# Issuing the scan's inverse and off-diagonal loads from GpSimd instead of SyncE, in a bidirectional DeltaNet / attention / MoE layer

## The chip, the cores and the metric

The kernel runs on one core of a Trainium2 chip. The metric is the device time of one execution, in microseconds (us): the median of three runs of the kernel before is 1728.37 us (1728.33 to 1729.34). The engines are TensorE (PE; PEld is its loading of weights), VectorE (DVE), ScalarE (ACT), GpSimd (POOL) and SyncE (SP). SP does no arithmetic; it issues transfers (DMAs). DMAs can also be issued by ACT and by POOL, and each of these engines works through its own instructions strictly in order.

## The reference

One layer of an encoder trunk, batch 1, 1024 tokens, width 1024, all in float32:

```python
h = rmsnorm(x) * (1 + scale1) + shift1            # shifts, scales, gates from silu(c) @ W_ada + b_ada
proj = h @ w_in                                   # attention q k v, DeltaNet q k v z, beta, decay, gates
A = block_attention(rope(q), rope(k), v)          # 8 query heads, 2 key heads, dim 64
B = gated_delta(fwd) + flip(gated_delta(bwd))     # 8 heads, dim 64, chunks of 64 tokens, 16 chunks
#   per chunk: T = inverse(I + L);  v_new = T@(b*(v - eg*k@state));  o = eg*q@state + a@v_new
#              state = gl*state + k^T@v_new       # sequential over the chunks
x = x + gate1 * ((sig(gA)*(A@Wa) + sig(gB)*(B'@Wd)) @ w_o)
x = x + gate2 * expert_choice_moe(rmsnorm(x) * (1 + scale2) + shift2)   # 16 experts, 128 tokens each
```

## The kernel before, in words

Large products are made of three matmuls over a high and a low part of each operand. The stages follow each other in this order: the first norm and its modulation, the projections for the DeltaNet, per-chunk matrices, the inversion of the 32x32 diagonal blocks on VectorE (`dn_invert`), the scan (about 370 to 715 us), the attention (to about 875 us), the up-projections with `w_o` and the routing, and the 16 experts.

**The scan.** `scan` runs 16 steps; step t treats chunk t forward and chunk 15 - t backward together. `scan_step` has the matmuls of lines 654, 669, 684 and 691 and the VectorE operations between them (658 to 693); line 687 writes the new state `Sc`, which line 654 of the next step needs. `scan_merge` puts the inverse of a chunk together from 32x32 blocks: line 630 multiplies an off-diagonal block (`nf`, loaded from `n_d`) with a transposed inverse (`wt`, from `wt_d`), line 637 multiplies the result with the inverse `w` (from `w_d`), line 639 writes it back into `w`, and line 669 uses `w`. The merge for step t + 1 runs within step t.

**Its loads.** `scan_load(t)` issues for each of the two directions two transfers of `w`, one of `nf` and one of `wt` (32 KB each, 256 pieces of 128 bytes), then in its second half `kq`, `kv` and `at`. For step t + 2 it is called in step t. `w` has two buffers; consecutive steps use different halves of the partitions of `nf` and `wt`. In the trace the tiles `nf` and `wt` share one allocation and are both named `Sc`; `w` is named `W`.

**What fills TensorE.** `late_fill` is a stream of 672 matmuls (line 1209: 14 groups of 48, for the remaining gates), of which `scan` hands out some after each part of a step, 35 a step as written:

```python
FILL = 8, 9, 9, 9, 60
```

Each group needs 512 KB of `w_in` (`wraw`, line 284, issued by POOL), which ACT (line 290) and VectorE (line 291) split into `wh` and `wl`. `attn_prep` (normalised and rotated q and k, one tile of 128 tokens a step, lines 739 to 809) runs beside steps 0 to 8; its `rope` table `tab` is multiplied on POOL (line 750). `mods_late` (lines 910 to 947; 40 VectorE operations of lines 930 and 932, each on a 256 KB load of `w_ada` issued by SP) comes behind it, and `scan_post` follows each step from step 8 on. After step 8, `attn_load` has POOL load 3.5 MB of keys, queries and values (lines 816 to 820).

**What sets the order.** The program is written in one order, but a scheduler puts each engine's instructions into the order in which, by its own estimates, they become ready. It also adds the waits. Each DMA of SP and ACT takes the next of eight counters, each DMA of POOL the next of eight others, and a DMA that takes a counter waits for the DMA that had it before.

Of the kernel before, what the change touches and what calls it, by code (L numbers as in the profile page):

```python
# [85 lines left out]
class K:  # L86
# [511 lines left out]
    def scan_load(self, t):  # L598


        nc = self.nc
        w = self.W[t % 2]
        nf, at, kv = self.nf, self.sa[:, t % 2], self.kv[t % 2]
        quads, ns = [], (t, 15 - t)
        kq = [self.kqs[d][:, t % 2] for d in range(2)]
        for d, n in enumerate(ns):
            x = n % 2
            src = self.w_d[d].rearrange("(n h) (b s c) -> n b s h c", h=8, b=2, s=32)
            for b in range(2):
                nc.sync.dma_start(w[64 * x + 32 * b:64 * x + 32 * b + 32, :, b * 32:b * 32 + 32], src[n, b])  # L610
            f, o = slice(64 * x + 32 * d, 64 * x + 32 * d + 32), slice(64 * x + 32 - 32 * d, 64 * x + 64 - 32 * d)
            nc.sync.dma_start(nf[f], self.n_d[d, n].rearrange("h s c -> s h c"))
            nc.sync.dma_start(self.wt[f], self.wt_d[d].rearrange("(n h) (c s) -> n c h s", h=8, s=32)[n])
            quads.append((f, o, slice(32 * d, 32 * d + 32), slice(32 - 32 * d, 64 - 32 * d)))
        yield w, at, kv, kq, nf, quads
        for d, n in enumerate(ns):
            r = slice(64 * (n % 2), 64 * (n % 2) + 64)
            nc.sync.dma_start(kq[d], self.kq_d[n])
            nc.sync.dma_start(kv[r], self.kv_d[n // 2, r])
            nc.sync.dma_start(at[r].rearrange("p h c -> p (h c)"), self.a_d[d, n // 2, r])  # L620
        yield
# [1065 lines left out]
```

## Time and profile before

| | |
|---|---|
| median of three runs | 1728.37 us |
| the profiled execution | 1728.42 us, its span 1726.6 us |
| granted TensorE clock, mean | 0.967 of full speed |
| busy: PE, DVE, ACT, POOL | 94%, 82%, 53%, 12% of the span |
| DMA traffic | 388.8 MB, 225 GB/s on average |

A timeline row gives start and length of a piece of work on an engine, and in brackets how long the engine had been idle and what ended that. In a row of windows, PEclk is the granted clock of TensorE as a share of full speed (1.0 is 2.4 GHz, 0.5 is 1.2 GHz), averaged over the stretch, and the DMA share is the mean busy share of the 16 DMA engines. "SPq" is SP's own queue of instructions.

### The profile page before, as it was taken

How to read it: one execution, taken by the hardware profiler on the slowest of the kernel's cores; microseconds unless marked ns; L12 is line 12 of the kernel's file. 1: busy time of each engine (PE TensorE's matmuls, PEld its weight loads, DVE VectorE, ACT ScalarE, POOL GpSimd, SP SyncE). 2: the span in 40 equal slices, each digit the busy share in tenths (PEclk: the TensorE clock that was granted, in tenths of full speed). 3: DMA queues.
4: the chain of work that ended last, by engine and by line, in shares of the span. 5: the costliest groups of instructions: out<-in, count | busy, mean ns of one | idle time of the engine just before them, and what ended most of it. 6: DMA issues, size and time to landing. Idle time of an engine off the chain costs nothing. (4 is left out here: it accounts for less than half of the span.)

```text
span 1726.6 us, 30147 instructions
## 1 busy us (share of the span) xinstructions
PE 1616.8 (94%) x11131; PEld 1278.1 (74%) x11131; DVE 1409.3 (82%) x2470; ACT 907.1 (53%) x1352; POOL 204.3 (12%) x196
## 2 busy tenths in 40 slices
PE   6999999889999899699999999669999999999997
PEld 4777778677777677478887788557777777777786
DVE  6899897954667757789986567979999999999996
ACT  6654432122344213288871323347777777777775
POOL 0000022010100100021112312300011000110000
PEclk9999999998999999699999999879999999999999
DMA  9454377257778966721135464769999999999981
GB/s 280 129 175 131 104 181 195 82 179 171 184 197 225 273 176 182 196 86 38 38 111 182 155 209 147 259 227 351 384 379 374 382 388 383 375 377 384 385 309 25
DMA packets 284146, 388.81 MB, mean 225 GB/s; under 512 B 88219, under 2 KB 152399, under 8 KB 283487
## 3 DMA queue, kind: packets, MB, share of 16 engines
q1 hardware_dynamic: 263279, 325.54, 57.4%
q0 software_dynamic: 14096, 48.77, 10.3%
q10 hardware_dynamic: 6624, 12.59, 2.0%
q8 instruction: 88, 1.44, 0.4%
q14 instruction: 59, 0.48, 0.1%
HBM read 328.04 MB, written 58.77 MB: 224 GB/s over the span
## 5 line engine op out<-in xcount | busy, mean ns | idle before, releaser
L1576 DVE TENSOR_TENSOR ew<-er,ew 128x1024 fp32r<-128x1024 f32 x384 | 452.2, 1219 | 29.8 <-ACT ew L1575 29.7
L1575 ACT CAST ew<-er 128x1024 fp32r<-128x1024 f32 x384 | 391.0, 1049 | 137.9 <-PE pj L1629 105.4
L1629 PE MATMUL pj<-ew,xT 128*128 128x512 f32 x1536 | 367.6, 396 | 4.5 <-DVE ew L1576 4.5
L1629 PEld LDWEIGHTS pj<-ew,xT 128*128 128x128 f32 x1536 | 283.2, 188 | 76.2 <-DVE ew L1576 19.5
L1646 PE MATMUL tr<-ew,aT 128*128 128x512 f32 x768 | 191.3, 398 | 0.0
L1646 PEld LDWEIGHTS tr<-ew,aT 128*128 128x128 f32 x768 | 139.7, 188 | 30.4 <-DVE ew L1576 3.4
L297 PE MATMUL pj<-hTh,wl 128*128 128x512 f32 (+1 forms) x384 | 123.4, 399 | 6.5 <-DVE wl L279 6.5
L297 PE MATMUL pj<-hTh,wh 128*128 128x512 f32 (+1 forms) x384 | 122.0, 397 | 3.3 <-ACT hTh L258 1.8
L297 PE MATMUL pj<-hTl,wh 128*128 128x512 f32 (+1 forms) x384 | 121.5, 397 | 1.4 <-DVE hTl L261 1.4
L297 PEld LDWEIGHTS pj<-hTh,wl 128*128 128x128 f32 (+1 forms) x384 | 71.9, 188 | 23.7 <-DVE wl L279 6.9
L297 PEld LDWEIGHTS pj<-hTh,wh 128*128 128x128 f32 (+1 forms) x384 | 70.7, 187 | 20.6 <-ACT hTh L258 1.9
L866 DVE TENSOR_REDUCE am<-pj 128x1 f32<-128x1024 f32 x64 | 77.7, 1216 | 10.0 <-PE pj L861 9.5
L1652 POOL DMA_INDIRECT out_dram<-xe,idxT x16 | 37.2, 2327 | 407.9 <-DVE tok L1550 353.4
L297 PEld LDWEIGHTS pj<-hTl,wh 128*128 128x128 f32 (+1 forms) x384 | 71.2, 187 | 18.6 <-DVE hTl L261 2.0
L1255 PE MATMUL pj<-hTh,uw 128*128 128x512 f32 x256 | 83.5, 404 | 1.0 <-DVE uth L1261 0.5
L868 ACT ACTIVATE ap<-pj,am 128x1024 f32<-128x1024 f32 x64 | 71.8, 1123 | 20.7 <-DVE am L866 11.1
L1209 PE MATMUL pj<-hTh,wh 128*128 128x512 f32 x224 | 79.9, 423 | 0.8 <-ACT y L1214 0.8
L1209 PE MATMUL pj<-hTh,wl 128*128 128x512 f32 x224 | 79.4, 422 | 0.0
L1209 PE MATMUL pj<-hTl,wh 128*128 128x512 f32 x224 | 77.8, 416 | 0.0
L861 PE MATMUL pj<-kT,qT 128*128 128x512 f32 x256 | 76.3, 406 | 0.0
L278 ACT CAST wh<-wraw 128x1024 fp32r<-128x1024 f32 (+1 forms) x26 | 26.7, 1028 | 87.9 <-PE pj L297 87.9
L325 DVE SCALAR_TENSOR_TENSOR y<-xc,colt,y 128x1024 f32<-128x1024 f32 x48 | 61.4, 1279 | 1.4 <-ACT y L323 0.9
(391 smaller groups left out, 2899.0 us busy)
## 6 DMA issues: line engine op xcount, KB each, us to landing
er<-in_w_gate_dram SPq DMA_DIRECT2D x128, 512.0 KB
er<-in_w_up_dram SPq DMA_DIRECT2D x128, 512.0 KB
er<-in_w_down_dram SPq DMA_DIRECT2D x128, 512.0 KB
wraw<-in_w_in_dram POOLq DMA_DIRECT2D x36, 512.0 KB, 5.9
mw<-in_w_ada_dram SPq DMA_DIRECT2D x44, 256.0 KB
wt<-in_w_ada_dram SPq DMA_DIRECT2D x16, 512.0 KB
gate_d<-y ACTq DMA_DIRECT2D x32, 256.0 KB
kqs<-kq_d SPq DMA_DIRECT2D x32, 256.0 KB
```

Source lines behind the costliest of these rows:

```text
L297: self.nc.tensor.matmul(ps[q][:n], w[:, k, :n], x[k][:, q * 512:(q + 1) * 512], start=(k == 0 and w is wh and x is self.hTh), stop=(k == 7 ...
L325: nc.vector.scalar_tensor_tensor(y, xc[:, t:t + S], w(t), y, op0=OP.mult, op1=OP.add)
L861: nc.tensor.matmul(ps[:, kh], qT[:, i * 128:(i + 1) * 128], self.kT[a][:, s, kh * 512:(kh + 1) * 512], start=(s == 0), stop=(s == 1), skip ...
L866: nc.vector.reduce_max(m, ps, axis=AX.X, negate=True)
L868: nc.scalar.activation(p, ps, AF.Exp, bias=m, scale=1.0, accum_out=self.rv[:, h, half * 4 + i:half * 4 + i + 1])
L1209: nc.tensor.matmul(ps[q], a[:, k], x[k][:, q * 512:(q + 1) * 512], start=(k == 0 and a is wh and x is self.hTh), stop=(k == 7 and a is wl))
L1255: nc.tensor.matmul(ps, w[:, k], v[k][:, qs], start=(k == 0 and p == 0), stop=(k == 3 and p == 2))
L1575: nc.scalar.copy(hi, raw)
L1576: nc.vector.tensor_sub(lo, raw, hi.bitcast(F))
L1629: nc.tensor.matmul(pg[m], x[:, 2 * kp + k], wi[:, k], start=(kp == 0 and k == 0 and n == 0), stop=(kp == 3 and k == 1 and n == 2))
L1646: nc.tensor.matmul(py[q], x[:, k], wi[:, q], start=(k == 0 and n == 0), stop=(k == 7 and n == 2))
L1652: nc.gpsimd.indirect_dma_start(out=out2, out_offset=bass.IndirectOffsetOnAxis(ap=self.idx[:, e:e + 1], axis=0), in_=y, in_offset=None, com ...
```

## The change

The four transfers per direction of `scan_load`'s first half are issued by POOL (`nc.gpsimd`) in place of SP (`nc.sync`): 8 a step, 128 in all. Their addresses and sizes stay.

```diff
--- before.py
+++ after.py
@@ -607,10 +607,10 @@
             x = n % 2
             src = self.w_d[d].rearrange("(n h) (b s c) -> n b s h c", h=8, b=2, s=32)
             for b in range(2):
-                nc.sync.dma_start(w[64 * x + 32 * b:64 * x + 32 * b + 32, :, b * 32:b * 32 + 32], src[n, b])
+                nc.gpsimd.dma_start(w[64 * x + 32 * b:64 * x + 32 * b + 32, :, b * 32:b * 32 + 32], src[n, b])
             f, o = slice(64 * x + 32 * d, 64 * x + 32 * d + 32), slice(64 * x + 32 - 32 * d, 64 * x + 64 - 32 * d)
-            nc.sync.dma_start(nf[f], self.n_d[d, n].rearrange("h s c -> s h c"))
-            nc.sync.dma_start(self.wt[f], self.wt_d[d].rearrange("(n h) (c s) -> n c h s", h=8, s=32)[n])
+            nc.gpsimd.dma_start(nf[f], self.n_d[d, n].rearrange("h s c -> s h c"))
+            nc.gpsimd.dma_start(self.wt[f], self.wt_d[d].rearrange("(n h) (c s) -> n c h s", h=8, s=32)[n])
             quads.append((f, o, slice(32 * d, 32 * d + 32), slice(32 - 32 * d, 64 - 32 * d)))
         yield w, at, kv, kq, nf, quads
         for d, n in enumerate(ns):
```

The scheduler also gives other engines another order. The rows below are each engine's own sequence.

TensorE at the end of the scan, before: from line 691 of step 14 to the first transposes of the attention (`ap`).

```order
L691 MATMUL dn<-st,sa 64x64 x16
L630 MATMUL tr<-Sc 32x32 x16
L684 MATMUL tr<-st,kv 64x64 x8
L654 MATMUL dn<-Sc,kqs 64x64
L637 MATMUL tr<-W,pt 32x32 x16
L654 MATMUL dn<-Sc,kqs 64x64 x31
L945 MATMUL tr<-macc,ones 1x512
L669 MATMUL dn<-st,W 64x64 x13
L149 MATMUL tr<-masks,st 128x128 x4
L669 MATMUL dn<-st,W 64x64 x3
L691 MATMUL dn<-st,sa 64x64 x16
L149 MATMUL dn<-masks,ap 128x128 x16
```

The same place now, from line 654 of the last step to its line 691:

```order
L654 MATMUL dn<-Sc,kqs 64x64 x26
L1209 MATMUL pj<-hTl_489,wh 128x512
L1209 MATMUL pj<-hTh_488,wl 128x512 x2
L1209 MATMUL pj<-hTh_529,wh 128x512 x2
L1209 MATMUL pj<-hTl_530,wh 128x512 x2
L1209 MATMUL pj<-hTh_529,wl 128x512 x2
L669 MATMUL dn<-st,W 64x64 x16
L1209 MATMUL pj<-hTh_570,wh 128x512 x2
L1209 MATMUL pj<-hTl_571,wh 128x512 x2
L1209 MATMUL pj<-hTh_570,wl 128x512 x2
L1209 MATMUL pj<-hTh_611,wh 128x512 x2
L691 MATMUL dn<-st,sa 64x64 x16
```

Before, the fill (line 1209) is used up when the last two steps run; now each step keeps about 35 of the 672, and 72 come after the last line 669. The steps in which the order before had more are, by the count of line 1209 between two lines 669, step 1 to 2 (76), 10 to 11 (57) and 11 to 12 (62). The four scores (line 861), which stood between steps 12 and 14, now stand behind the last step, 12 or 13 fills apart.

POOL around `attn_load`, before:

```order
L284 DMA wraw<-in_w_in_dram 128x8x128
L750 TENSOR_TENSOR tab<-rp,rw 128x128 x2
L284 DMA wraw<-in_w_in_dram 128x8x128
L816 DMA kT_6104<-kT_d 128x2x1024
L818 DMA qT_6106<-qT_d 128x512
L818 DMA qT_6107<-qT_d 128x512
L819 DMA vS<-vS_d 128x8x256
L820 DMA kT_6105<-kT_d 128x2x1024
L284 DMA wraw<-in_w_in_dram 128x8x128
```

and now:

```order
L612 DMA Sc<-n_d 32x8x32
L613 DMA Sc<-wt_d 32x8x32
L816 DMA kT_6104<-kT_d 128x2x1024
L818 DMA qT_6106<-qT_d 128x512
L818 DMA qT_6107<-qT_d 128x512
L819 DMA vS<-vS_d 128x8x256
L820 DMA kT_6105<-kT_d 128x2x1024
L610 DMA W<-w_d 32x8x32 x4
L612 DMA Sc<-n_d 32x8x32
L613 DMA Sc<-wt_d 32x8x32
L612 DMA Sc<-n_d 32x8x32
L613 DMA Sc<-wt_d 32x8x32
```

What moved: the four loads of `w` for step 11 and the `nf` and `wt` of step 12 stand behind `attn_load`; in front of it are the `w` of step 10 and the `nf` and `wt` of step 11. Two loads of `wraw` that stood before the first `tab` now stand behind the loads for steps 0 to 2, and from there on a `wraw`, a pair of `tab` or both stand between the loads of most steps and the next. On VectorE, 16 of the 40 operations of `mods_late` now stand in steps 1 to 3, beside `attn_prep`; before, all stood in step 8 and later.

## Rows read from the trace of the kernel before

**Rows 1.** The page: busy tenths of TensorE in 40 equal slices of the span.

```profile
PE   6999999889999899699999999669999999999997
```

**Rows 2.** Windows of the scan: us, PE, PEld, DVE, ACT, POOL busy, PEclk, DMA share, GB/s.

```profile
382.50:390.00 7.50, 2.58 (x8) 1.33 (x6) 0.77 (x2) 0.60 (x1) 0.66 (x1) 0.79 0.84 168
390.00:400.00 10.00, 9.35 (x89) 6.55 (x93) 0.00 (x0) 1.48 (x4) 0.87 (x2) 0.50 1.01 201
...
466.70:541.90 75.20, 72.63 (x1125) 56.49 (x1125) 53.62 (x146) 32.62 (x72) 6.21 (x11) 1.00 0.81 216
566.00:574.00 8.00, 7.88 (x104) 6.75 (x104) 6.32 (x19) 4.08 (x7) 0.00 (x0) 0.79 0.62 167
598.00:606.00 8.00, 0.55 (x4) 0.15 (x3) 3.39 (x14) 0.53 (x1) 0.00 (x0) 0.75 0.89 258
606.00:612.00 6.00, 6.00 (x16) 4.51 (x15) 0.75 (x1) 0.00 (x0) 0.00 (x0) 0.50 0.93 241
690.00:730.00 40.00, 24.56 (x319) 17.34 (x315) 30.55 (x68) 8.43 (x16) 0.00 (x0) 0.66 0.73 191
```

**Rows 3.** Timeline of PE: start, length, line, tile, [idle before <-releaser].

```profile
387.12 0.28 PE L630 MATMUL tr<-Sc 32*32 32x32 f32 x2 [4.32 <-DMA Sc<-wt_d]
...
390.65 1.02 PE L630 MATMUL tr<-Sc 32*32 32x32 f32 x30 [1.25 <-DMA Sc<-wt_d]
...
605.90 0.28 PE L630 MATMUL tr<-Sc 32*32 32x32 f32 x2 [7.45 <-DMA Sc<-wt_d]
...
693.45 0.68 PE L684 MATMUL dn<-st,kv 64*64 64x64 f32 x16 [2.94 <-DVE st L674]
```

**Rows 4.** Waits of SP's queue, 360 to 400 us: us in total, times, longest.

```profile
SPq L613 <- DMA rw<-in_k_norm_w_dram: 2.2, 1, 2.2
SPq L612 <- DMA rw<-in_k_norm_w_dram: 2.0, 1, 2.0
```

**Rows 5.** Timeline of SP: start, length, line, transfer.

```profile
592.53 4.40 SPq L612 DMA_DIRECT2D Sc<-n_d  x1
```

**Rows 6.** Line 610's DMAs on SP: ns min/median/max, first and last start.

```profile
L610 SPq DMA_DIRECT2D W<-w_d x64: 303/443/1682, 377.2 to 694.9; - x64
```

**Rows 7.** Line 525's DMAs on POOL, and their landing.

```profile
L525 POOL DMA_DIRECT2D n_d<-nn x32: 582/582/600, 226.4 to 293.3; - x32
...
DMA to landing us min/median/max: 1.9/2.9/5.7
```

**Rows 8.** Windows again: the stretch in which line 525 issues.

```profile
200.00:300.00 100.00, 99.27 (x891) 78.31 (x891) 84.95 (x159) 29.96 (x48) 23.88 (x38) 1.00 0.67 169
```

**Rows 9.** DMA issues on POOL: KB each, median us to landing.

```profile
wraw<-in_w_in_dram POOLq DMA_DIRECT2D x36, 512.0 KB, 5.9
...
kT<-kT_d POOLq DMA_DIRECT2D x2, 1024.0 KB, 10.2
```

**Rows 10.** Timeline of POOL: the first load of attn_load, and a `wraw`.

```profile
587.27 0.70 POOL L816 DMA_DIRECT2D kT<-kT_d  x1 [11.10 <-DMA st<-in_w_ada_dram]
...
596.92 0.90 POOL L284 DMA_DIRECT2D wraw<-in_w_in_dram  x1 [6.22 <-DVE wl L291]
```

**Rows 11.** Waits over the whole span: us in total, times, longest.

```profile
POOL wraw L284 <- DVE wl L291: 81.3, 6, 18.6
```

**Rows 12.** Timeline of PE: starts of line 669 in steps 4, 5, 9, 10.

```profile
486.61 1.15 PE L669 MATMUL dn<-st,W 64*64 64x64 f32 x32
...
505.45 1.15 PE L669 MATMUL dn<-st,W 64*64 64x64 f32 x32
...
574.60 1.15 PE L669 MATMUL dn<-st,W 64*64 64x64 f32 x32
...
589.07 1.15 PE L669 MATMUL dn<-st,W 64*64 64x64 f32 x32
```

**Rows 13.** Line 930 on DVE, and a wait before it.

```profile
L930 DVE SCALAR_TENSOR_TENSOR macc<-mw,cs,macc x15: 732/744/751, 566.1 to 717.7; 128x512 f32<-128x512 f32 x15
...
  DMA st<-in_w_ada_dram: 5.7, 1
```

## The prediction

> **What bounds the kernel now.** I read the slices of the whole span first. Each is 43.2 us; apart from the first and the last, TensorE is under nine tenths in six of them: the eighth, ninth, 14th and 17th (302 to 388, 561 to 604, 690 to 734 us), which hold the scan's beginning, middle and end, and the 26th and 27th, ahead of the experts [rows 1]. Then I read windows of the scan, then TensorE's own timeline for what ended its idle times, and last the queues of SP and POOL for what had been late.
>
> In the middle of the scan TensorE is the bound: 72.6 us of 75.2 are busy at full clock, while VectorE is busy for 53.6 [rows 2]. What can be won lies in four places where TensorE stands idle or, just after, is granted less than the full clock. I count a place as its idle time plus busy time times the missing share of the clock, all from [rows 2]:
>
> - start, 382.5 to 400: 4.92 + 2.58 x 0.21 + 0.65 + 9.35 x 0.50 = 10.8 us;
> - 566 to 574: 0.12 + 7.88 x 0.21 = 1.8 us;
> - 598 to 612: 7.45 + 0.55 x 0.25 + 6.00 x 0.50 = 10.6 us;
> - end of the scan and start of the attention, 690 to 730: 15.44 + 24.56 x 0.34 = 23.8 us.
>
> Together 47.0 us. At the first and the third place the wait is for a load of the scan: line 630 waits 4.32, 1.25 and 7.45 us for `wt` [rows 3]. At the end it is not: line 684 of the last steps waits for VectorE (2.94 us) [rows 3], because no fill is left to lie between a step's links. The clock rows show the same order each time: TensorE stood still, and afterwards worked at a granted 0.50 (1.2 GHz) for six to ten us [rows 2].
>
> Why the loads are late can be read on SP. Two of the first loads waited 2.2 and 2.0 us for transfers of `rw` that have nothing to do with them [rows 4]: the wait for the counter that the earlier transfer still holds. Before the wait at 605.90 one issue alone took SP 4.40 us [rows 5], where a load of this size usually takes 0.44 [rows 6].
>
> **What leaves SP.** 128 issues x 0.443 us = 57 us of SP [rows 6]. Nothing computes on SP, so this is worth nothing by itself; it counts only through loads that start earlier, and these are in the places above.
>
> **What comes to POOL.** No row shows such a load issued from POOL. The nearest is the store of `n_d`, the same 256 pieces of 128 bytes in the other direction: 582 ns each [rows 7]. I take it; 128 x 0.582 = 74.5 us, 4.7 us a step. From both sides: not below the 0.30 us of SP's shortest [rows 6], and as an upper end the 0.90 us of a `wraw` with its 512 KB [rows 10], 38 to 115 us in all. A step lasts 18.84 us in the first half (35 fills, from step 4 to 5) and 14.47 us with 31 fills in the second (from step 9 to 10) [rows 12], so POOL has room at either end, and I charge nothing. The landing I bound by 2.9 us (`n_d`, [rows 7]) and 10.2 us (1 MB of `kT`, [rows 9]) and take 2.9, nearest in size.
>
> A rule speaks against this place. VectorE was busy for 85 of the 100 us in which most of the 32 stores of `n_d` were issued, and their issue stayed within 582 to 600 ns [rows 7, 8]. The Trainium skill (DMA: Bandwidth & Descriptors, SWDGE vs HWDGE vs iDMA) says that GpSimd writes the descriptors of its DMAs into SBUF and can be locked out there by VectorE in some modes, which SP's DMAs are immune to. By that rule the issues would lengthen beside a busy VectorE; these rows show no lengthening, and the sum keeps 582 ns.
>
> **The four places, one by one.**
>
> Start. POOL's last load for step 0 stands behind the store of `wt_d`, as on SP, but not behind `rw` or `kq`. The place costs between 0 (all landed in time) and 10.8 us (as late as before). With five issues of 0.58 us and 2.9 us landing instead of SP's waits I take 2.
>
> 598 to 612. The load that was late was `wt`, issued on SP among other transfers, while the attention's 3.5 MB moved. Now the `nf` and `wt` of step 11 stand before `attn_load` in POOL's order, and behind it only the `w` of step 11 and the `nf` and `wt` of step 12. Three of the `w` can be issued at once; the next waits for the counter of the first 1 MB load, 10.2 us [rows 9]. Issue and landing of five loads behind the last 1 MB load, which may end some 3 us later than 10.2 because five issues precede it, make about 10 + 3 + 5 x 0.58 + 2.9 = 19 us. The first use of `w`, line 637 of step 11, comes, by the order of the matmuls, about a step and two thirds after POOL is through with step 10's loads (an estimate: 14.47 x 1.67 = 24 us), and the `nf` of step 12 a step later still. So I take 0; the upper end is the old 10.6. In that row the first of these loads itself had waited 11.10 us [rows 10], and now the `w` of step 11 would wait with it: that is the upper end's case.
>
> Order of TensorE. The fill is spread at about 35 a step to the last step, and 72 lie behind it with the scores between them. The total of matmuls is the same. In the last two steps fill lies where the idle time was; behind them the attention still has to start: its first exponentials, transposes and the last `scan_post` follow each other. Of the 23.8 us I keep a third, 8 (between 0 and 23.8).
>
> First steps. In steps 1 to 3 VectorE gets 16 operations of `mods_late` at 0.744 us [rows 13]: 11.9 us in three steps, beside 53.6 / 4 = 13.4 a step [rows 2]. That makes 17.4 a step against 18.84 [rows 12], so VectorE gets as full as TensorE and the order decides; I take 2 us a step, 6 (0 to 11.9). The same 11.9 us are missing in steps 8 to 15, where that gives VectorE air but no time, for TensorE bounds there.
>
> Small waits, with the 1.8 us at 566, go on in the new order: 5 (0 to 10).
>
> **The sum.** 47.0 - (2 + 0 + 8 + 6 + 5) = 26 us less. From the profiled execution's 1728.42 us (span 1726.6 and 1.8 around it; 0.05 above the median, so nothing has to be converted): 1702.4, I say 1702. Every stage behind the scan keeps its length: the later stages have the same instructions, and a shift of the scan's end shifts them whole. With the lower ends of all terms it would be 1681, with the upper ends (10.8 + 10.6 + 23.8 + 11.9 + 10 = 67) 1748; all of them at one end is unlikely.
>
> **Rivals.**
>
> *The loads stay late.* If a load takes from POOL as long as the transfers around it, the start (10.8) and the wait beside the attention's loads (10.6) stay, and only the order gains: 47.0 - (10.8 + 10.6 + 8 + 6 + 5) = 6.6, so 1722. For it: both waits fell into stretches with the DMA engines 84 to 101% busy [rows 2], and POOL's 1 MB loads took 10 us there [rows 9]. Against it: 4.40 us of issue and the waits on `rw` were SP's own [rows 4, 5]. The Trainium skill says the same as this rival (DMA: Bandwidth & Descriptors, Issuing engines are not separate DMA queues): the DMAs of all issuers share 16 engines, and a second issuer saves only issue time. By that rule alone the 57 us of SP's issue would be the whole effect, and little of them is on the path.
>
> *POOL's order holds the loads up (slower).* Each load of a step now stands behind a `wraw` that waits for VectorE's line 291; before, POOL waited there up to 18.6 us, six times, 81.3 in total [rows 11], with nothing behind it. A `w` can be issued after line 669 of step t and is used about a step and a third later (an estimate: 19 to 25 us); 4 issues and a landing take 5.2. So the wait decides from 14 to 20 us on. If it does so in 6 of the 11 `wraw` that stand among the loads, each for 4 us and 3 us of lost clock after it (as 7.45 brought 3.0 at 606), it is 42 us: 1702 + 42 = 1744. Against it: `wraw` waits so long because it stands ready early; the scheduler has put it behind the loads at a point where it expects line 291 done.
>
> *VectorE becomes the bound in steps 1 to 3 (slower).* Each of the 16 early operations waits for a load of `w_ada`, and VectorE is in order; one such wait took 5.7 us [rows 13]. From 26 / 16 = 1.6 us each on, the gain is gone; at 3 us each it is 48 for the 6: 1744 too. Against it: the loads run four ahead, and only one such wait before was long.
>
> **How the numbers follow.** The forecast with its own range of 1687 to 1716 gets 0.62, the loads that stay late 0.20, POOL's order 0.08, VectorE 0.05, and 0.05 an even end in which gains and new waits cancel. About 0.2% (3.5 us) is what a measurement of this kernel can tell. Faster by more: 0.62 + 0.18 = 0.80; within it 0.02 + 0.05 = 0.07; slower 0.08 + 0.05 = 0.13. For 8 in 10 the range has to take in the rival at 1722 and a little of both ends: 1686 to 1729.
>
> **What would show it.** Right: line 630 waits for no DMA at the start nor near 600 us, TensorE works through the last two steps at a granted clock near 1.0, line 669 comes about every 18 us and then every 15 to 16, and the attention's last matmul and all behind it come about 26 us earlier. Wrong on the loads: line 630 or 637 still waits for `Sc` or `W`. Wrong on the order: VectorE busy over 95% in steps 1 to 3, or POOL's timeline with a long idle time in front of a `wraw` and the loads of a step close behind it while TensorE waits.

## The result, and the profile after

The changed kernel takes 1705.92 us (median of four runs, 1704.01 to 1707.41), the kernel before beside it 1728.72; the ratio is 0.9867 (95% interval 0.985 to 0.9884), so 23 us less. The forecast was 1702, 26 us less, and the range holds the time. The way there is another one than the prediction's: of the waits that it wanted to see go, 3 us net went. The other 21 us are time in which TensorE was busy at full clock before and no longer is.

Two lines of each page say so before any stage is looked at: TensorE's busy time, and the slices that answer to [rows 1]. Before:

```profile
PE 1616.8 (94%) x11131; PEld 1278.1 (74%) x11131; DVE 1409.3 (82%) x2470; ACT 907.1 (53%) x1352; POOL 204.3 (12%) x196
```

After:

```profile
PE 1591.9 (93%) x11131; PEld 1269.2 (74%) x11131; DVE 1407.3 (83%) x2470; ACT 906.1 (53%) x1352; POOL 288.9 (17%) x324
PE   5999999897799889999999999579999999999997
```

The same 11131 matmul records are busy for 24.9 us less at the same mean clock (0.967), and the busy share falls. A kernel that had only lost waits would show the same busy time in a shorter span. In the slices (42.6 us each now) the hole at the end of the scan, the 17th, is filled; the one at its beginning lies in the tenth now, the one in the middle in the 14th and 15th, and the eleventh has a new one.

**Stalls and work.** The scan and the attention lie between the first fill matmul (369.0 us before, 371.6 after; the 2.6 us arise in the first 100 us, where this execution was granted less clock) and the first matmul of the up-projections (891.7 and 870.2): 522.7 and 498.6 us, 24.1 less. In windows of 2 us I split this into stalls, counted as in the prediction (idle time plus busy time times the missing clock), and work (busy time times the granted clock). The windows of the whole places, after:

```profile
380.00:412.00 32.00, 23.79 (x348) 19.23 (x347) 12.84 (x36) 6.68 (x16) 11.95 (x22) 0.84 0.78 180
412.00:480.00 68.00, 56.65 (x890) 45.80 (x892) 50.63 (x125) 25.04 (x54) 25.27 (x39) 0.85 0.96 254
556.00:640.00 84.00, 71.28 (x1150) 54.80 (x1149) 58.42 (x146) 15.87 (x32) 24.61 (x40) 0.94 0.92 248
676.00:740.00 64.00, 60.42 (x335) 47.13 (x336) 45.25 (x67) 43.68 (x79) 10.30 (x8) 1.00 0.33 104
```

and before (the other places are in [rows 2]):

```profile
380.00:412.00 32.00, 26.43 (x287) 19.40 (x286) 10.66 (x27) 6.43 (x14) 1.75 (x3) 0.79 0.76 160
412.00:480.00 68.00, 66.65 (x975) 52.16 (x976) 44.43 (x115) 25.36 (x57) 6.23 (x10) 1.00 0.66 171
560.00:620.00 60.00, 51.33 (x797) 39.26 (x796) 36.77 (x93) 12.58 (x25) 5.23 (x7) 0.89 0.89 250
686.00:740.00 54.00, 38.07 (x450) 28.07 (x440) 43.88 (x88) 19.27 (x38) 2.85 (x3) 0.75 0.69 190
```

| us | before | after | forecast | measured |
|---|---|---|---|---|
| start, 380 to 412 | 11.5 | 12.5 | -8.8 | +1.0 |
| steps 1 to 3, 412 to 480 | 1.3 | 17.6 | +6.0 | +16.3 |
| beside the attention's loads (560 to 620; 556 to 640) | 13.5 | 16.1 | -10.6 | +2.6 |
| end of the scan (686 to 740; 676 to 740) | 24.9 | 3.6 | -15.8 | -21.3 |
| elsewhere | 5.2 | 3.6 | +3.2 | -1.6 |
| stalls in all | 56.4 | 53.4 | -26.0 | -3.0 |
| work | 466.4 | 445.3 | 0 | -21.1 |

**Where the work went.** A step of before and one of after, both at full clock. Before, step 5 (from 505.45 to 524.05, 37 fills), some rows of TensorE's timeline:

```profile
507.65 0.68 PE L684 MATMUL dn<-st,kv 64*64 64x64 f32 x16
508.27 0.51 PE L1209 MATMUL pj<-hTl,wh 128*128 128x512 f32 x1
508.70 0.97 PE L691 MATMUL dn<-st,sa 64*64 64x64 f32 x26
...
514.93 0.68 PE L684 MATMUL tr<-st,kv 64*64 64x64 f32 x16
515.54 0.50 PE L1209 MATMUL pj<-hTl,wh 128*128 128x512 f32 x1
...
519.77 0.63 PE L1209 MATMUL pj<-hTh,wl 128*128 128x512 f32 x2
520.24 0.62 PE L1209 MATMUL pj<-hTh,wh 128*128 128x512 f32 x2
...
524.05 1.15 PE L669 MATMUL dn<-st,W 64*64 64x64 f32 x32
```

After, step 6 (35 fills); the rows of line 684 go on alternating to 522.67:

```profile
518.42 1.15 PE L669 MATMUL dn<-st,W 64*64 64x64 f32 x32
...
522.19 0.27 PE L684 MATMUL dn<-st,kv 64*64 64x64 f32 x1
522.20 0.27 PE L684 MATMUL tr<-st,kv 64*64 64x64 f32 x1
...
522.71 1.10 PE L691 MATMUL dn<-st,sa 64*64 64x64 f32 x32
523.74 0.69 PE L637 MATMUL tr<-W,pt 32*32 32x32 f32 x32
...
534.33 1.15 PE L669 MATMUL dn<-st,W 64*64 64x64 f32 x32
```

Read from start to next start, not by the length in the row, since matmuls overlap. The 32 records of line 684 cost 0.62 + 0.61 = 1.23 us before, in two groups into the tiles `dn` and `tr` that stand 7 us apart. After, they alternate and cost 522.71 - 522.19 = 0.52. A fill inside a run costs 0.235 us (519.77 to 520.24 for two); the one that stands alone at 508.27 costs 0.43. Over the scan, by line and weighted with the clock: line 684 takes 16.9 us before and 7.8 after, the fill 173.6 and 166.7, line 654 21.0 and 18.7, the transposes of line 149 24.0 and 21.3. The fill stood in 107 runs and stands in 69: 7.0 / 38 = 0.18 us for each run less. By line these differences make up the 21.1 us; only the alternation is varied by itself below (e1). The whole step takes 18.60 us before, 0.61 of it idle, and 15.91 after, with two fills fewer and otherwise the same matmuls.

The Trainium skill (TensorEngine Tiling (Array Packing), Tiling Modes) says that a change of the tiling mode drains TensorE, while tiles of one mode work independently; fill and scan use 128x128 and 64x64 or 32x32 tiles, and 0.18 us for each run of fill agrees with that. It can't be the only reason: after, a lone fill between transposes, which use the same 128x128 mode, takes 0.48 us as well (515.33 to 515.81). The Trainium skill also says (TensorE: Matmul & The Clock Gate, The mechanism) that a weight load overlaps a matmul in flight only in another row group. The matmuls into `dn` all have one, those into `tr` the other, and alternating they take 16 ns a record instead of 39.

The row group alone doesn't explain that. By the code, lines 669 and 691 change it at every matmul too, and their records cost 34 and 32 ns (518.42 to 519.50; 522.71 to 523.74). What differs is the number of tiles of the array, given by the partitions that a matmul reads and those that it writes: lines 669, 691 and each separate half of line 684 go to two 64x64 tiles, the alternating line 684 and line 654 to four, and line 654 costs 17 ns a record (64 records from 529.29 to 530.38, after). So two tiles go with 32 to 39 ns and four with 16 to 17. No run varies the number of tiles by itself.

**What TensorE waits for now.** Rows of its timeline, after, that answer to [rows 3]:

```profile
391.05 1.06 PE L630 MATMUL tr<-Sc 32*32 32x32 f32 x30 [5.44 <-DMA Sc<-wt_d]
433.27 1.12 PE L149 MATMUL tr<-masks,kk 128*128 128x128 f32 x4 [7.49 <-DVE Sc L687]
463.11 1.09 PE L149 MATMUL tr<-masks,hl 128*128 128x128 f32 x4 [3.86 <-DVE hl L795]
587.38 1.97 PE L669 MATMUL dn<-st,W 64*64 64x64 f32 x32 [6.19 <-issue]
608.28 1.97 PE L669 MATMUL dn<-st,W 64*64 64x64 f32 x32 [3.19 <-issue]
```

and of VectorE's, in front of them:

```profile
431.64 0.75 DVE L930 SCALAR_TENSOR_TENSOR macc<-st,cs,macc 128x512 f32<-128x512 f32 x1 [6.10 <-DMA st<-in_w_ada_dram]
457.13 0.75 DVE L930 SCALAR_TENSOR_TENSOR macc<-st,cs,macc 128x512 f32<-128x512 f32 x1 [3.31 <-DMA st<-in_w_ada_dram]
582.97 0.75 DVE L720 SCALAR_TENSOR_TENSOR dz<-tr,colt,dz 128x512 f32<-128x512 f32 x1 [6.07 <-DMA sa<-a_d]
605.17 0.75 DVE L930 SCALAR_TENSOR_TENSOR macc<-mb,cs,macc 128x512 f32<-128x512 f32 x1 [3.94 <-DMA mb<-in_w_ada_dram]
```

Each of the four later waits begins on VectorE: an operation of `mods_late` or `scan_post` that nobody needs yet waits for its load, and the scan's operations stand behind it. (Line 720 doesn't use the `sa` that is named there; the only load it needs is the one of `dz_d`, and in e9 the trace names that.) Only the first wait is still one for `wt`.

POOL's side, its loads and one wait that answers to [rows 11]:

```profile
L610 POOL DMA_DIRECT2D W<-w_d x64: 582/582/700, 371.3 to 644.4; - x64
DMA to landing us min/median/max: 2.2/4.3/11.7
```

```profile
L613 POOL DMA_DIRECT2D Sc<-wt_d x32: 582/582/585, 378.4 to 631.8; - x32
DMA to landing us min/median/max: 2.8/5.9/10.9
```

```profile
POOL wraw L284 <- DVE wl L291: 6.7, 2, 5.7
```

### The profile page after: what moved, and what is told of

Its sections match the earlier page's. It is cut to its first block, busy times and chain, and to the rows that moved or that the text cites. A ratio compares the mean times of both kernels' runs of the same rounds, so it can differ in the third digit from the quotient of the medians.

```text
span 1705.6 us, 30198 instructions
## 1 busy us (share of the span) xinstructions
PE 1591.9 (93%) x11131; PEld 1269.2 (74%) x11131; DVE 1407.3 (83%) x2470; ACT 906.1 (53%) x1352; POOL 288.9 (17%) x324
## 5 line engine op out<-in xcount | busy, mean ns | idle before, releaser
L297 PEld LDWEIGHTS pj<-hTl,wh 128*128 128x128 f32 (+1 forms) x384 | 71.3, 188 | 18.7 <-DVE hTl L261 2.0
L1209 PE MATMUL pj<-hTh,wl 128*128 128x512 f32 x224 | 74.8, 408 | 0.0
L275 POOL DMA_DIRECT2D wraw<-in_w_in_dram x23 | 20.6, 897 | 263.4 <-DVE wl L279 194.7
```

Of the source, the lines that this page charges most:

```text
L297: self.nc.tensor.matmul(ps[q][:n], w[:, k, :n], x[k][:, q * 512:(q + 1) * 512], start=(k == 0 and w is wh and x is self.hTh), stop=(k == 7 ...
L1209: nc.tensor.matmul(ps[q], a[:, k], x[k][:, q * 512:(q + 1) * 512], start=(k == 0 and a is wh and x is self.hTh), stop=(k == 7 and a is wl))
```

## The experiments

Stalls and work of all runs, in the same stretch and windows; "before" was 1728.7 to 1730.8 beside them.

| kernel | us | ratio (95%) | idle | clock | work |
|---|---|---|---|---|---|
| before | 1728.7 | 1 | 36.7 | 19.6 | 466.4 |
| changed | 1705.9 | 0.9867 (0.985 to 0.9884) | 39.5 | 13.8 | 445.3 |
| e1 unpaired | 1714.0 | 0.9902 (0.9885 to 0.9918) | 41.3 | 11.0 | 449.7 |
| e2 on ScalarE | 1715.9 | 0.9919 (0.9904 to 0.9934) | 49.4 | 16.4 | 445.2 |
| e3 mods held | 1702.1 | 0.9838 (0.9821 to 0.9854) | 36.7 | 13.3 | 444.9 |
| e4 attn spread | 1706.1 | 0.9855 (0.9836 to 0.9875) | 36.5 | 18.0 | 445.3 |
| e5 others to POOL | 1721.2 | 0.9957 (0.994 to 0.9974) | 49.8 | 17.3 | 445.1 |
| e6 w only | 1710.7 | 0.9885 (0.9869 to 0.9902) | 44.8 | 16.1 | 449.5 |
| e7 nf, wt only | 1716.6 | 0.9925 (0.9908 to 0.9942) | 48.2 | 11.8 | 450.4 |
| e8 held, spread | 1700.9 | 0.9827 (0.9811 to 0.9843) | 36.1 | 12.9 | 445.8 |
| e9 changed again | 1707.4 | 0.9864 (0.9847 to 0.9881) | 39.0 | 13.8 | 445.0 |
| e10 start on ACT | 1700.8 | 0.9829 (0.9812 to 0.9846) | 38.0 | 14.3 | 444.4 |
| e11 post to POOL | 1697.3 | 0.9795 (0.9778 to 0.9812) | 35.0 | 11.6 | 444.5 |
| e12 all to POOL | 1721.4 | 0.9946 (0.993 to 0.9963) | 45.4 | 17.4 | 447.3 |

**e1: line 684 not alternating.** In the changed kernel:

```diff
-            for h in range(8):
-                hr = slice(64 * (h % 2), 64 * (h % 2) + 64)
-                for d, r in enumerate(rs):
+            for d, r in enumerate(rs):
+                for h in range(8):
+                    hr = slice(64 * (h % 2), 64 * (h % 2) + 64)
```

> The changed kernel with the two loops around line 684 exchanged, so that a step's matmuls into the tile dn come first and those into tr behind them, as the order before mostly had them; all else in TensorE's order stays but for a few places. Density theory (TensorE's matmuls themselves take less time in the new order): alternating, the 32 records of a step take 0.52 us from start to next start (522.19 to 522.71 in the trace of the changed kernel), apart 2 x 0.62 = 1.24; 15 x 0.72 = 10.8 us more, between 8 and 11: 1714 to 1717. Stall theory (the gain is waiting time and half clock saved): the loads stay on GpSimd and the waits stay, so 1704 to 1708.

Measured: 1714.0 us, 7 more than the changed kernel (e9). Of this 4.4 are work: line 684 takes 10.8 us in place of 7.8, line 691, which now mixes with it, 17.8 in place of 16.8. The profiled execution was among its shortest (1710.6), so the rest is not in the trace. The stall theory (1704 to 1708) falls. The density theory holds in kind, but its size was too large: the work grew by 4.4 us, not by 8 to 11, and the time reaches the lower end of its range with the help of what the trace doesn't show. In the order before the two halves also stand apart, with other work between. Together but not alternating they cost 3.0 us more than alternating; the other 6.1 of the 9.1, by the difference, come from standing apart.

**e2: the loads on ScalarE.** The changed lines with `nc.scalar` in place of `nc.gpsimd`.

> The same 128 loads issued by ScalarE instead, neither SyncE nor GpSimd. TensorE's order comes out nearly as in the changed kernel (69 runs of fill in place of 107, line 684 alternating in nearly all of its matmuls). Order theory (what counts is that SyncE is relieved and the order that follows from it): within 5 us of the changed kernel, 1701 to 1711, although the loads are issued elsewhere. GpSimd theory (GpSimd's own queue and its eight counters make the difference; ScalarE shares SyncE's counters): loads late again, 1720 to 1730.

Measured: 1715.85 us, between the two forecasts, and the split tells why. The work is 445.2, as in the changed kernel to 0.1 us: the order came, and with it the whole gain in work. The stalls are 12.5 us larger: ScalarE's own work stands behind its loads, and TensorE behind that. ScalarE's timeline with the lengths of its issues (ns), then TensorE's:

```profile
422.97 8.05 ACTq L610 DMA_DIRECT2D W<-w_d  x4
431.06 0.59 ACT L807 CAST qst<-tr 128x512 fp32r<-128x512 f32 x1 [8.05 <-DMA W<-w_d]
...
585.84 0.36 ACT L639 COPY W<-tr 32x256 f32<-32x256 f32 x1 [16.22 <-DMA W<-w_d]
...
L610 ACTq DMA_DIRECT2D W<-w_d x64: 309/338/1810, 375.0 to 657.0; - x64
```

```profile
431.70 1.06 PE L637 MATMUL tr<-W,pt 32*32 32x32 f32 x32 [4.54 <-ACT qst L807]
...
591.23 1.09 PE L149 MATMUL tr<-masks,st 128*128 128x128 f32 x4 [12.10 <-DVE st L714]
```

The four issues at 422.97 take 0.31 us each. In the rest of the 8.05 us ScalarE waits: by the semaphores of the trace each of the last three goes out when a transfer of SyncE lands that had its counter before (a store of line 1217, loads of `kq` and `qraw`). So the rival was right that ScalarE shares SyncE's counters, but it cost a part of the gain, not all of it.

**e5: the other loads to GpSimd.** In the kernel before, `kq`, `kv` and `at` (lines 618 to 620) are issued by `nc.gpsimd`, and the loads of this change stay on SyncE.

> The kernel before with the three other loads of a step (kq, kv and at, 6 a step) issued by GpSimd, while the loads of this change stay on SyncE. TensorE's order again comes out like that of the changed kernel (74 runs of fill in place of 107, line 684 alternating, ten operations of mods_late in steps 2 and 3). Order theory: TensorE's own work between 360 us and the first matmul of the up-projections, 475 us at full clock before and 457 after, comes out between 455 and 460 though the loads in question have not moved, and the time between 1702 and 1714. Theory that it is these loads' own lateness that the change mends: work stays near 475 and the time at 1725 to 1732.

Measured: work 445.1 (in the narrower stretch of the table; 454.2 in the one of the expectation, just below its 455 to 460) although none of the loads in question moved. So the gain in work comes with the order in which TensorE's instructions stand once SyncE is relieved, not with these loads' arrival. The time, 1721.24, lies above the forecast. On SyncE one load of `nf` alone took 8.64 us to issue, and VectorE stood for 11.81 us:

```profile
565.86 8.64 SPq L612 DMA_DIRECT2D Sc<-n_d  x1
```

```profile
588.32 0.75 DVE L720 SCALAR_TENSOR_TENSOR dz<-tr,colt,dz 128x512 f32<-128x512 f32 x1 [11.81 <-DMA W<-w_d]
```

The first is not the reason of the second. Line 720 doesn't use the `W` that is named; it waits for `dz_d`, whose two loads SyncE had issued in front of that `nf` (from 563.32, 2.44 us for both). By their counters the later one landed just before 588.3, over 22 us after its issue. Why it took so long is not shown.

**e6 and e7: half the change.** Only `w` (line 610) on GpSimd, and only `nf` and `wt` (lines 612, 613).

> Only the four loads of w a step (64 of the 128) on GpSimd; nf and wt stay on SyncE. In the order 73 runs of fill, line 684 alternating in 194 of 240 matmuls, and mods_late stays out of steps 1 to 6. Order theory: the work falls to 457 to 462 us, and without the stop of VectorE in steps 1 to 3 (17.7 us lost there in the changed kernel) the time is between 1692 and 1704, below the changed kernel's. Theory of the late loads (nf and wt were the late ones, and they stay on SyncE): 1722 to 1732. Half the loads, half the gain: 1715 to 1720.

> The counterpart: only nf and wt on GpSimd, w stays on SyncE. 71 runs of fill, line 684 alternating in 194 of 240, mods_late out of steps 1 to 5. Order theory: as with w alone, 1692 to 1704, and within 5 us of it. Theory of the late loads (nf and wt alone matter): as the changed kernel, 1703 to 1710. Half the loads, half the gain: 1715 to 1720.

Measured: 1710.67 and 1716.57 us. The work falls by 16.9 and 16.0 of the 21.1 us, in step with the alternating part of line 684 (194 of 240) and the runs of fill (73 and 71). The time does not come out at 1692 to 1704: without the stop in steps 1 to 3 other waits are larger, 11.6 us for `dz_d` at line 720 in e7 and 10.1 for one load of `w_ada` in e6. The theory that `nf` and `wt` alone matter falls: e7 is the slower one. Its time lies in the range of "half the loads, half the gain", but not for that reason: it has three quarters of the gain in work, and the waits took the rest.

**e3: mods_late held.** In the changed kernel:

```diff
             elif t == 7:
+                for y in self.mw + [self.macc[:, g] for g in range(2)]:
+                    self.nc.vector.tensor_copy(y[:, 0:1], self.Sc[:, 0, 0:1])
                 behind.append(self.mods_late(MODG, 8))
```

> The changed kernel with the 40 operations of mods_late held back: before it starts, five copies of one column of Sc into its buffers, so that none of its loads or operations can move ahead of step 7 (none stands before step 8 now). VectorE theory: in steps 1 to 3 VectorE stood still for 1.5, 6.1 and 3.3 us at line 930 or 932 for loads of w_ada, and TensorE lost 17.7 us to idle time and clock between 420 and 470 us where the kernel before lost 1.3; 10 to 16 of it come back: 1690 to 1696. Rival (attn_prep and the rope table on GpSimd hold steps 1 to 3, not mods_late): within 3 us, 1703 to 1709. A third (what is held back stands in the way at the end of the scan, as before): 1710 to 1716.

Measured: 1702.05 us, 5 less than e9, where 10 to 16 were expected. Steps 1 to 3 are clean, and the stretch beside the attention's loads is worse. Windows of this kernel:

```profile
412.00:480.00 68.00, 67.15 (x1191) 54.38 (x1190) 58.04 (x156) 34.30 (x77) 31.97 (x49) 1.00 0.97 255
556.00:640.00 84.00, 67.28 (x1075) 50.45 (x1077) 59.86 (x139) 14.76 (x29) 21.68 (x37) 0.88 0.93 243
```

Stalls at 412 to 480: 17.6 before the edit, 0.8 now. From 480 to 640: 17.9 and 32.2. SyncE, TensorE and VectorE show how:

```profile
551.98 7.75 SPq L703 DMA_DIRECT2D dz<-dz_d  x2
563.06 2.07 SPq L919 DMA_DIRECT2D mw<-in_w_ada_dram  x2
```

```profile
567.79 0.75 DVE L930 SCALAR_TENSOR_TENSOR macc<-mw,cs,macc 128x512 f32<-128x512 f32 x1 [7.10 <-DMA mw<-in_w_ada_dram]
```

```profile
576.44 1.09 PE L149 MATMUL tr<-masks,st 128*128 128x128 f32 x4 [11.79 <-DVE st L714]
```

So the early `mods_late` is what stopped steps 1 to 3, and the same loads stop the scan where they are put instead.

**e4: attn_load in three pieces.** A `yield` before lines 819 and 820, and:

```diff
             if t == 8:
                 sta.close()
-                self.attn_load(self.pool(sta, "attn", side="right"))
+                parts = self.attn_load(self.pool(sta, "attn", side="right"))
+            if t in (8, 10, 12):
+                next(parts, None)
```

> The changed kernel with attn_load in three pieces, the first 1 MB and the queries after step 8 as now, the values after step 10 and the second 1 MB after step 12, so that they stand behind the scan's loads for step 11 and 12 on GpSimd. Traffic theory: at 565 us SyncE took 7.9 us for two loads of dz_d while the 3.5 MB moved, VectorE waited 6.1 us for one of them at line 720 and TensorE 6.2 us behind that, and 1 us more at half clock; with half of it gone from there 5 to 8 us come back: 1698 to 1701. Counter theory of the prediction's upper end (the scan's loads behind the 1 MB loads wait for their counters): the two waits of 4.3 and 3.0 us on GpSimd go, but nothing waited for these loads: 1704 to 1708.

Measured: 1706.08 us, no gain that can be told from e9. The mechanism is there: the two loads of `dz_d` took SyncE 2.38 us instead of 7.87, and VectorE's long wait for `dz_d` is gone. But between 556 and 640 the idle time fell from 12.7 to 10.2 us while the clock loss rose from 3.4 to 7.5, and the waits for `w_ada` stayed. The traffic theory was right on the wait and wrong on the time.

**e8: both.** mods_late held and attn_load in three pieces.

> The changed kernel with mods_late held back to step 7 and attn_load in three pieces, together. With mods_late alone held, SyncE took 7.75 us for two loads of dz_d at 552 us while attn_load's 3.5 MB moved, loads of w_ada came out behind that, VectorE waited 7.1 and 3.6 us for them and TensorE 11.8. Traffic theory: with two thirds of attn_load moved on, 6 to 10 us of that go: 1692 to 1697. Queue theory (SyncE's order alone makes w_ada late, whatever else moves): 1700 to 1705.

Measured: 1700.9 us, the same as e3 within its interval: 21.5 us of VectorE's waits for `w_ada` are left, in shorter pieces. The queue theory's number.

**e9: the changed kernel again.**

> The changed kernel once more, beside the next three, so that they can be set against it on the same chip. By its earlier ratio to the kernel before, 0.9867 x 1730 = 1707 (1704 to 1710). TensorE's own work 445 us again by the order theory, within 1; idle time and clock loss, 39.5 and 13.8 us in its first trace, may come out 3 us apart.

Measured: 1707.38 us; work 445.0, stalls 52.7. The waits at line 669 are 8.46 and 2.13 us here, 6.19 and 3.19 in the first trace.

**e10: step 0 from ScalarE.** On the kernel of e8, `scan_load` issues the eight loads of step 0 by `nc.scalar`.

> mods_late held and attn_load spread, and the eight loads of step 0 alone issued by ScalarE, which has almost nothing to do at 375 us; TensorE's order stays. In the changed kernel the two wt of step 0 were issued by GpSimd at 378.5 and 380.7 us and line 630 had both at 391; from 380 to 384 us the DMA engines were busy for 0.16 of the time. Landing theory (the loads issued by GpSimd start late, the engines being free): line 630 goes on 3 to 6 us earlier, the 12 us lost between 380 and 412 fall to about 6, and 1692 to 1698. Store theory (the wait for the store of wt_d and the traffic behind it set the start, whoever issues): 1699 to 1704.

Measured: 1700.76 us, as e8. The stalls from 380 to 412 are 15.0 in place of 12.4: the landing theory falls. On ScalarE the second `wt` went out at 387.33 and the first, issued at 378.21, was waited for until 389.09, as long as from GpSimd:

```profile
378.21 0.41 ACTq L613 DMA_DIRECT2D Sc<-wt_d  x1
...
387.33 0.31 ACTq L613 DMA_DIRECT2D Sc<-wt_d  x1
```

```profile
389.09 0.31 PE L630 MATMUL tr<-Sc 32*32 32x32 f32 x2 [7.12 <-DMA Sc<-wt_d]
```

**e11 and e12: less on SyncE.** On the kernel of e8, lines 703 and 722 of `scan_post` by `nc.gpsimd` (e11); `kq`, `kv` and `at` by `nc.gpsimd` (e12).

> mods_late held and attn_load spread, and scan_post's loads of dz_d and stores of dn_d (lines 703 and 722, four a step from step 8 on) issued by GpSimd in place of SyncE. With them on SyncE, VectorE waited 21.5 us for loads of w_ada, issued by SyncE behind stores that wait for VectorE's line 720. SyncE-order theory: these waits fall to under 10 us and the time to 1690 to 1696. Traffic theory (w_ada is slow because of what moves beside it): 1698 to 1704. Against both: GpSimd now stands at the stores, and the loads of w and wt behind them come late: 1706 to 1716.

> mods_late held and attn_load spread, and also kq, kv and at on GpSimd (14 loads a step there, 8.1 us at 0.58), so that SyncE has none of the scan's loads. SyncE-order theory: the waits for w_ada fall as in the kernel beside it, 1690 to 1697. Traffic theory: 1698 to 1704. Against both: 14 loads in one order, each waiting for another line of TensorE, hold each other up, as moving kq, kv and at alone had given only half the gain: 1706 to 1716. By the order theory TensorE's work stays between 445 and 448 us in any case (74 runs of fill, 214 of 240 alternating).

Measured: e11 1697.26 us, the best kernel here, 10 us below the changed kernel on the same chip (e9). That its reason is SyncE's order is not shown: VectorE still waits 19.9 us for `w_ada`, where under 10 were expected; the longest of the four rows:

```profile
DVE macc L932 <- DMA st<-in_w_ada_dram: 7.8, 5, 2.6
```

Against e8 its stalls are 2.4 and its work 1.3 us less, and the runs overlap (1692.6 to 1699.3; 1697.6 to 1702.9). e12 went the other way, 1721.44, above the ranges of all three theories. The last one (1706 to 1716) has the direction but not the reason: after step 0 TensorE waits for none of the 14 loads. It waits for VectorE, 18.3 us in all at line 714's result (17.1 in e11):

```profile
PE tr L149 <- DVE st L714: 18.3, 6, 6.7
```

VectorE's waits for `w_ada` are 23.3 us there, although SyncE has none of the scan's loads left, so the SyncE-order theory falls. Against e11, 16.2 us of stalls and 2.8 of work are more in the stretch. The largest stops that e11 doesn't have stand at line 669, 4.14 and 5.38 us, behind VectorE again (1.25 and 1.34 in e11). What makes e12 24 us slower than e11 at much the same waits for `w_ada` stays open.

## Why the prediction was right in the number and wrong in the reason

- *What bounds the kernel.* "In the middle of the scan TensorE is the bound: 72.6 us of 75.2 are busy at full clock" was taken to mean that nothing is to be won there. This is the step that failed first: a busy TensorE was taken for a full one. The order of its instructions was compared in the forecast, and only for where the fill stands, not for how often fill and small matmuls change places and whether line 684 alternates. By line that makes up the 21.1 us; e2, e3 and e5 show the same 445 us with the loads on three different engines.
- *Start, "I take 2".* Measured 12.5. GpSimd was free, but the first `wt` had to wait for the store of `wt_d` (6.01 us, to 378.45), and the first three `wt` landed 6.8 to 10.3 us after their issue, not 2.9. e10 shows that another issuer does not help. The rival "the loads stay late" was right here in the result but not in its reason, busy DMA engines: they were busy for 0.16 of the time from 380 to 384.

```profile
378.45 0.58 POOL L613 DMA_DIRECT2D Sc<-wt_d  x1 [6.01 <-DMA wt_d<-wtmp]
```

- *598 to 612, "So I take 0".* The wait for `wt` is gone, as forecast; the place is not. VectorE's wait for `dz_d`, behind SyncE's 7.87 us at 565.12, took its place, 16.1 us of stalls in all. The prediction asked what is late next among the loads that moved, not among those that stayed on SyncE.
- *First steps, "I take 2 us a step, 6".* The place was right, size and mechanism were not: 16.3, above the upper end of 11.9. It was sized by VectorE's busy time (11.9 us of work); what came were the waits of an in-order VectorE for `w_ada` (1.54, 6.10, 3.31 us), which the third rival had named and given 0.05. e3 confirms it.
- *End, "I keep a third, 8".* Measured 3.6. The spread fill does cover the last two steps, better than forecast: 21.3 us of stalls gone.
- *What comes to POOL.* 582 ns an issue, 582 at the median and 700 at most in line 610. The landing, bounded by 2.9 and 10.2 us, was taken at the lower end; the medians are 4.3 and 5.9. This costs nothing after the start, since the loads are early.
- *POOL's order holds the loads up.* It didn't: the waits of `wraw` for line 291 are 6.7 us in place of 81.3 [rows 11], and line 637 waits for no load.
- *The signs that it named.* Line 630 still waits at the start (5.44 us), but not near 600. From step 4 on line 669 comes every 15 to 17 us, apart from two steps of 22 and 21. The up-projections begin 21.5 us earlier, not 26. The sign for steps 1 to 3, VectorE busy over 95%, stayed away (50.6 of 68 us) although the stop came: an engine that stands waiting for a load is not busy.

So the sum of stalls missed by 23 us (26 forecast, 3 found) and the work that the sum did not contain by 21, in the other direction. That the time fell into the range is to a large part chance. The clean part is the end of the scan: it alone is worth 21.3 us, and the new stop in steps 1 to 3 takes 16.3 of them back.

## What to carry to other kernels

Where an edit moves instructions, count in TensorE's order how often matmuls of different tile sizes change places and how many different tiles of the array consecutive small ones go to (two or four here), and price it from start to next start: busy time is not work done. Where a queue is relieved, look for the in-order engine whose spare work is now taken in earlier, and ask for each such operation whether its load can be there. Split every comparison into idle time, clock and work before giving a reason: here the time moved as if the forecast were true, and only the split showed that it wasn't.

## What was not expected of the hardware

- An issue of these loads on GpSimd kept its 0.58 us through all traffic (0.84 at most, in e9), while a single one on SyncE took up to 4.40 us [rows 5] and 8.64 (e5), with the DMA engines busy throughout. Full engines are not the only case: in e10 one on ScalarE took 4.59 us from 379.81 on, with the engines busy for 0.12 of the time from 380 to 384.
- TensorE's work repeats far better than its waits: 444.4 to 445.8 us in nine executions of eight kernels in which line 684 alternates (nearly) throughout and the fill stands in 69 to 74 runs, while idle time went from 35.0 to 49.8.
- From 380 to 384 us, with loads of GpSimd issued from 378.45 on and not landed, the DMA engines were busy for 0.16 of the time. Why these take 7 to 10 us to land is open. It is no matter of GpSimd alone: e10's first `wt` on ScalarE took as long, and the kernel before has the same quiet stretch, 0.07 from 380 to 384.

```profile
380.00:384.00 4.00, 4.00 (x19) 3.34 (x18) 0.94 (x2) 1.54 (x2) 3.05 (x6) 1.00 0.16 33
```
